# Seven products for a fourth k pair in three FFN down parts, and a tile of sums in the first FFN parts

## The chip, the cores and the metric

The kernel runs on one core of one Trainium2 chip. The metric is the device time of a run in microseconds (us). A core has five engines that run side by side and wait for each other by semaphores: TensorE (PE, matmuls; its weight loads are listed as PEld), VectorE (DVE), ScalarE (ACT), GpSimd (POOL) and SyncE (SP, which here only issues DMAs). VectorE and ScalarE carry out their instructions in the order in which they are written, and so does the DMA queue of SyncE.

## What is computed

A trunk of two layers over 256 positions and 2048 features, in float32. Each layer has a mixer (sliding-window attention and mLSTM in the first, forgetting attention in the second) and a feed-forward net (FFN) of hidden size 5632; the change lies in the FFN alone:

```python
def swiglu(xn, w_gate, w_up, w_down):
    return (jax.nn.silu(xn @ w_gate) * (xn @ w_up)) @ w_down

    for layer in range(DEPTH):
        ...
        h = h + mix.astype(h.dtype)
        h = h + swiglu(rms_norm(h, norm_ffn[layer]), w_gate[layer], w_up[layer], w_down[layer])
    return rms_norm(h, norm_final)
```

## The kernel before

**Products of float32 from two halves.** Every operand is split into a high part and the rest: ScalarE casts (`hi`), VectorE subtracts (`lo`), as in `split_chunk` (L188, L189) and `split_plain` (L357, L358). One product of a 128x128 block of activations (kept in TensorE) with 128x512 weights (streamed) is three matmuls, `three` (L533 to L535): high by high, high by low, low by high.

**Tiles.** Activations are cut into k tiles of 128 features (x in `xh`, `xl`; the FFN's inner values in `mh`, `ml`) and two halves of 128 positions, t0 and t1. Weights are loaded by SyncE in raw tiles of 128 x 2 x 512 float32, 512 KB, which are two neighbouring k tiles (a k pair) of one matrix and 512 of its columns. Split weights go into `hi`/`lo` slots; `slot` hands out eight of them in turn during the FFN.

**A group.** `pair_group` computes two blocks of 512 columns at once: gate and up in a gate/up group, two neighbouring blocks of the output in a down group. It walks over k pairs in a given order, a list of (kind, pair). A pair of kind 0 is plain: two raw tiles, each split whole, and 2 x 2 x 2 = 8 products, 24 matmuls. A pair of kind 1 is mixed: its four blocks of activations and four of weights go through a scheme of the Strassen-Winograd kind, with seven products, 21 matmuls, for which sums of weight blocks and sums of activation blocks are needed. The sums of activations for a pair (`sums_of`) are made once, kept in `sx` or `sd`, and used by every group of the part; both have room for three pairs. A fourth mixed pair exists in four gate/up groups (`HEAVY` for the groups in `DENSE`: 4, 5, 8, 9); its sums lie in `x4` and in the t1 halves of `xh` and `xl` that mixed pairs leave unused, since the scheme reads only t0 of a pair's first k tile. The products that belong to both output blocks gather in four banks of PSUM (`prods`), the others in four more (`plain`); `combine` adds the first up at the end of the last mixed pair, and the two sets of banks change places from group to group.

**Weight sums of a mixed pair**, with raw tiles ra and rb of two k tiles each: ra is split; rb's first half becomes ra's plus rb's first half, by VectorE (L606) in the first part and by an accumulating DMA on POOL's queue (L600) in the others (`adding`); rb is split; L608 and L610 make the other three sums in place in rb and ra; those are split in two steps. Raw tiles of mixed pairs come from a pool with five buffers (`RAWS`), those of plain pairs from one with four (`wr`). `pair_group` has a second form of the sums, with other slots (`halves`), that the mixers use.

**The FFN's stages.** `ffn` runs three parts: gate/up groups 0 to 2, 3 to 6 and 7 to 10, each followed by two down groups (output blocks 0 and 1, then 2 and 3) over the part's 12 or 16 k tiles. The orders are `ORDER` or `HEAVY` for gate/up, `DOWN` for down: two mixed pairs of six in the first part, three of eight in the others (1, 3 and 5). The last part of layer 1 has only its first down group in this form. The output of a gate/up group (SiLU, product) is turned by transposing DMAs on SyncE's queue (L709); `join` then splits it into `mh`, `ml` and makes the sums of its mixed pairs. `join` is due at position 6 of the next gate/up group (`MID`), or at position 5 of the first down group (`MID_DOWN`); so the two last k pairs of a down group come last in its order. The first part's last group is turned on TensorE instead. After a down group its sums are added to h (L768) and then the four plain banks (`close`, L371).

**What sets the order.** The program is written in this order, and a scheduler places each engine's instructions ahead of time by its own estimate of durations, so neighbouring pairs' instructions are interleaved on TensorE, VectorE and ScalarE. On the chip each engine keeps to that order.

Of the kernel before, what the change touches and what calls it, by code (L numbers as in the profile page):

```python
# [24 lines left out]
CK = 2  # L25
# [17 lines left out]
    8: ((0, 0), (1, 1), (0, 2), (1, 3), (0, 4), (1, 5), (0, 6), (0, 7)),  # L43
}
MID = 6
MID_DOWN = 5
# [8 lines left out]
LATER_DOWN = (5, 6)  # L55
RAWS = 5
P_JOIN = 4
# [19 lines left out]
def trunk(  # L77
# [48 lines left out]

    loaded = [None]

    def load_raw(w, k0, c0, n, pool=wr, bufs=4, raws=None):
# [134 lines left out]
    def sums_of(pool, sh, sl, copies, full=None, tags=("tmp", "tmp"), bufs=None, box=None, x4=None):  # L264
        if box is not None:
            full, s = box[:, 0:4, :].rearrange("p (i t) q -> p i t q", i=2), box[:, 4:8, :]
            copies(full.rearrange("p i t q -> p i (t q)"))
        elif full is None:
            full = pool.tile([P, 2, NT, P], F32, tag=tags[0], name="full", bufs=bufs)
            copies(full.rearrange("p i t q -> p i (t q)"))  # L270
        if box is None:
            s = pool.tile([P, 4, P], F32, tag=tags[1], name="s4", bufs=bufs)
        nc.vector.tensor_tensor(out=s[:, 0, :], in0=full[:, 0, 1, :], in1=full[:, 1, 1, :], op=ALU.add)
        nc.vector.tensor_tensor(out=s[:, 1, :], in0=s[:, 0, :], in1=full[:, 0, 0, :], op=ALU.subtract)
        nc.vector.tensor_tensor(out=s[:, 2, :], in0=full[:, 0, 1, :], in1=full[:, 0, 0, :], op=ALU.subtract)
        nc.vector.tensor_tensor(out=s[:, 3, :], in0=full[:, 1, 0, :], in1=s[:, 1, :], op=ALU.subtract)
        if x4 is None:
            split_plain(sh, sl, s)
        else:
            split_plain(sh, sl, s[:, 0:3, :])  # L280
            split_plain(x4[:, 0, :], x4[:, 1, :], s[:, 3, :])
# [63 lines left out]
    def scrap(fp, n):  # L345
# [194 lines left out]
    def pair_group(fp, par, lhs, sums, mats, order, todo=(), halves=None, inner=None, raws=None, adding=False):  # L540
# [32 lines left out]
        for pos, (kind, pair) in enumerate(order):  # L573
# [72 lines left out]
    def ffn(layer, fp, sx, x4, sd, key, todo, idx_next=None, key_next=None, finish=None):  # L646
        r = rstd(key)

        def sums_x(pair):
# [5 lines left out]
        for g0, g1 in zip(PARTS, PARTS[1:]):  # L655
            end = g1 == PARTS[-1]
            nk = 4 * (g1 - g0)
            order = DOWN[nk // 2]
            for g in range(g0, g1):
# [50 lines left out]
                def join(c=c, turned=turned, g=g, g0=g0, order=order):  # L710
                    ct = c[:, 0:2, :].rearrange("p a n -> p (a n)")
# [7 lines left out]
                    for half in range(2):  # L719
                        pair = 2 * (g - g0) + half  # L720
                        if pair in mixed_of(order):
                            j = mixed_of(order).index(pair)
                            sums_of(
                                fp,
                                sd[0][:, j, :, :],
                                sd[1][:, j, :, :],
                                None,
# [24 lines left out]
            for n0 in (0, 2):  # L752
                if end and idx_next is None and n0 == 2:
# [5 lines left out]
                plain, c = pair_group(  # L759
                    fp, 1 - n0 // 2, m_of, sums_d, [(wd, n0 * NB), (wd, (n0 + 1) * NB)], order, todo, adding=g0 >= ADDING  # L760
                )
# [12 lines left out]
    def close_layer(layer, w_out, idx, key, **rest):  # L774
        with tc.tile_pool(name=f"fp{layer}", bufs=2) as fp:
            nx = len(mixed_of(ORDER))
            nd = max(len(mixed_of(o)) for o in DOWN.values())
            sx = [fp.tile([P, nx, 4, P], F32R, name=f"sx{i}", bufs=1) for i in range(2)]
            x4 = fp.tile([P, 2, P], F32R, name="x4", bufs=1)
            todo = out_proj(w_out, idx, key, (*sx, x4, fp))  # L780
            sd = [fp.tile([P, nd, 4, P], F32R, tag=f"sd{i}", name=f"sd{i}", bufs=1) for i in range(2)]
            more = [[fp.tile([P, CK, NB], F32R, name=f"{a}{i}", bufs=1) for a in ("hi", "lo")] for i in range(2)]
            stock.extend(more + [slot() for _ in range(6)])
            ffn(layer, fp, sx, x4, sd, key, todo, **rest)
            stock.clear()


# [599 lines left out]
```

## Time and profile before

| | |
|---|---|
| median of 3 runs | 2088.28 us (2087.98 to 2088.78) |
| the profiled execution's own time | 2086.12 us |
| its span, first to last instruction | 2084.4 us |
| its mean granted TensorE clock | 0.996 |

The profile is of one execution. Its page gives busy times of the engines (the share of the span in which at least one instruction of the engine was under way), the chain of work that ended last, and groups of instructions with their mean duration. A window's row gives, after the length of the stretch, the busy time of TensorE, its weight loads, VectorE, ScalarE and POOL with the number of instructions, then the granted clock, the share of the DMA engines and GB/s. Timeline rows give start, length, engine, line and tiles, and in brackets the idle time before and what ended it. Records of one engine can overlap: an instruction's start, not its end, then tells what it costs.

### The profile page before, as it was taken

The numbers are of one execution on the slowest core, as the hardware profiler recorded it, in microseconds if no ns is written. First come the engines' busy times: TensorE is split into PE (matmuls) and PEld (weight loads), VectorE is DVE, ScalarE is ACT, GpSimd is POOL, SyncE is SP. The second block draws the span as 40 slices with busy tenths as digits, with TensorE's granted clock in tenths as the row PEclk, the third lists the DMA queues.
The fourth block names the chain that finished last, engine by engine and source line by source line (L and its number), as shares of the span: only waits on it lengthen the run. The fifth ranks groups of instructions, "written<-read, shape, count | busy, mean of one in ns | idle before, by whom it ended". The sixth has DMA issues, their size and how long they took to land.

```text
span 2084.4 us, 26995 instructions
## 1 busy us (share of the span) xinstructions
PE 2066.4 (99%) x9449; PEld 1713.1 (82%) x9449; DVE 1804.5 (87%) x2235; ACT 1383.7 (66%) x1760; POOL 113.2 (5%) x143
## 2 busy tenths in 40 slices
PE   9999999999999999999999999999999999999998
PEld 7878887887888888888888888888878888888887
DVE  6788768999899998998899688679998999899994
ACT  6777677765567656767677776687655677557763
POOL 1010000000000000000010000000000000000000
PEclk9999999999999999999999999999999999999999
DMA  8566577666778777778676766587657777867864
GB/s 292 175 208 197 189 252 227 187 204 213 210 225 265 232 233 237 226 240 218 205 211 208 229 198 185 155 265 227 222 174 235 236 220 239 259 205 209 265 206 150
DMA packets 320664, 455.07 MB, mean 218 GB/s; under 512 B 107644, under 2 KB 115856, under 8 KB 320400
## 3 DMA queue, kind: packets, MB, share of 16 engines
q1 hardware_dynamic: 307088, 426.27, 64.9%
q0 software_dynamic: 12720, 25.99, 6.8%
q8 instruction: 74, 1.21, 0.2%
q10 hardware_dynamic: 720, 1.09, 0.2%
q14 instruction: 62, 0.51, 0.1%
HBM read 428.87 MB, written 2.12 MB: 207 GB/s over the span
## 4 chain that ended last, share of the span: by engine, by line
PE 86%; DMA 4%; DVE 4%; ACT 4%; issue 3%; SPq 0%; ACTq 0%; POOLq 0%; POOL 0%; DVEq 0%
PE acc L533 19%; PE acc L534 19%; PE acc L535 19%; PE prod L533 5%; PE prod L534 5%; PE prod L535 5%; PE acc L224 4%; PE acc L223 4%; PE acc L225 4%; DVE lo L189 1%; DMA raw<-in_w_down_dram 1%; ACT hi L188 1%; DMA raw<-in_w_gate_dram 1%; PE p L387 1%; ACT box L323 1%
## 5 line engine op out<-in xcount | busy, mean ns | idle before, releaser
L189 DVE TENSOR_TENSOR lo<-raw,hi 128x1024 fp32r<-128x1024 f32 (+3 forms) x648 | 762.7, 1192 | 148.5 <-ACT hi L188 146.2
L188 ACT CAST hi<-raw 128x1024 fp32r<-128x1024 f32 (+3 forms) x648 | 654.0, 1027 | 352.9 <-PE acc L535 130.1
L534 PE MATMUL acc<-lo,xh 128*128 128x512 f32 x1272 | 495.0, 390 | 0.0
L535 PE MATMUL acc<-hi,xl 128*128 128x512 f32 x1272 | 493.9, 390 | 0.0
L533 PE MATMUL acc<-hi,xh 128*128 128x512 f32 x1272 | 480.5, 391 | 2.4 <-ACT hi L188 2.4
L357 ACT CAST hi<-raw 128x1024 fp32r<-128x1024 f32 (+1 forms) x323 | 286.9, 894 | 193.7 <-DVE raw L608 78.2
L358 DVE TENSOR_TENSOR lo<-raw,hi 128x1024 fp32r<-128x1024 f32 (+1 forms) x323 | 328.3, 1026 | 31.2 <-ACT hi L357 30.4
L533 PEld LDWEIGHTS acc<-hi,xh 128*128 128x128 f32 x1272 | 239.4, 188 | 53.6 <-ACT hi L188 4.0
L534 PEld LDWEIGHTS acc<-lo,xh 128*128 128x128 f32 x1272 | 239.6, 188 | 49.7 <-issue 0.2
L535 PEld LDWEIGHTS acc<-hi,xl 128*128 128x128 f32 x1272 | 239.3, 188 | 49.9
L534 PE MATMUL acc<-lo,mh 128*128 128x512 f32 x466 | 181.4, 390 | 0.0
L535 PE MATMUL acc<-hi,ml 128*128 128x512 f32 x466 | 180.8, 389 | 0.0
L533 PE MATMUL acc<-hi,mh 128*128 128x512 f32 x466 | 176.3, 389 | 4.4 <-ACT hi L357 4.4
L610 DVE TENSOR_TENSOR raw<-raw 128x1024 f32<-128x1024 f32 x103 | 125.6, 1220 | 0.9
L224 PE MATMUL acc<-lo,mh 128*128 128x512 f32 (+1 forms) x322 | 126.3, 392 | 0.0
L223 PE MATMUL acc<-hi,mh 128*128 128x512 f32 (+1 forms) x322 | 125.8, 391 | 0.0
L225 PE MATMUL acc<-hi,ml 128*128 128x512 f32 (+1 forms) x322 | 123.7, 391 | 0.0
L533 PEld LDWEIGHTS acc<-hi,mh 128*128 128x128 f32 x466 | 87.5, 188 | 23.0 <-ACT hi L357 4.9
L534 PEld LDWEIGHTS acc<-lo,mh 128*128 128x128 f32 x466 | 87.6, 188 | 18.2
L535 PEld LDWEIGHTS acc<-hi,ml 128*128 128x128 f32 x466 | 87.6, 188 | 18.2
L224 PE MATMUL acc<-lo,xh 128*128 128x512 f32 (+3 forms) x288 | 99.9, 347 | 0.2 <-DVE lo L189 0.2
L225 PE MATMUL acc<-hi,xl 128*128 128x512 f32 (+3 forms) x288 | 98.8, 344 | 0.0
(362 smaller groups left out, 3033.1 us busy)
## 6 DMA issues: line engine op xcount, KB each, us to landing
raw<-in_w_gate_dram SPq DMA_DIRECT2D x176, 512.0 KB, 5.3
raw<-in_w_up_dram SPq DMA_DIRECT2D x176, 512.0 KB, 5.2
raw<-in_w_down_dram SPq DMA_DIRECT2D x176, 512.0 KB, 5.7
raw<-in_w_in_odd_dram SPq DMA_DIRECT2D x88, 512.0 KB, 5.1
raw<-in_w_in_even_dram SPq DMA_DIRECT2D x51, 512.0 KB, 4.7
raw<-in_w_out_even_dram SPq DMA_DIRECT2D x32, 512.0 KB, 5.1
raw<-in_w_out_odd_dram SPq DMA_DIRECT2D x32, 512.0 KB, 4.7
raw<-in_w_gate_dram POOLq DMA_DIRECT2D x56, 256.0 KB, 5.7
```

Of the source, the lines that this page charges most:

```text
L188: latest[0] = nc.scalar.copy(hi[:, k, 0:n], raw[:, k, 0:n])
L189: nc.vector.tensor_tensor(out=lo[:, k, 0:n], in0=raw[:, k, 0:n], in1=hi[:, k, 0:n].bitcast(F32), op=ALU.subtract)
L223: nc.tensor.matmul(o, ah[:, ts], hi, start=(k == 0), stop=False)
L224: nc.tensor.matmul(o, ah[:, ts], lo, start=False, stop=False)
L225: nc.tensor.matmul(o, al[:, ts], hi, start=False, stop=(k == k_all - 1 and cs.stop == n))
L323: nc.scalar.copy(ju[:, :, b], turned[:, b, :, :, :].rearrange("p k t q -> p (k t q)"))
L357: nc.scalar.copy(dst_h, src)
L358: nc.vector.tensor_tensor(out=dst_l, in0=src, in1=dst_h.bitcast(F32), op=ALU.subtract)
L533: nc.tensor.matmul(o, ah, hi, start=start, stop=False)
L534: nc.tensor.matmul(o, ah, lo, start=False, stop=False)
L535: nc.tensor.matmul(o, al, hi, start=False, stop=stop)
L610: nc.vector.tensor_tensor(out=ra, in0=ra, in1=both, op=ALU.subtract)
```

## The change

Two edits, both in the FFN.

**First parts (groups 0 to 2 and their down groups, both layers).** The five raw tiles are no longer taken in turn from a pool but made once (`ring`). In the first parts four of them take the raw weights, and the fifth is a tile of sums, `t4`. The sums of weights are made in another way: rb's second half is split at once; two sums go to `t4`, two to ra; `t4` and ra are then each split whole. The sums are the same four as before. The later parts go on with `adding` and five raw tiles in turn. The box for turning h in the output projection (`scrap`, n = 1) uses two tiles of the ring.

**Down groups of three later parts** (both in layer 0, the first of the two in layer 1): the order becomes `DOWN_MORE`, with four mixed pairs of eight, 1, 3, 4 and 5. The sums of activations of pair 4 are written to the t1 halves of k tiles 2, 6, 8 and 10 of `mh` and `ml` (`MORE_ROOMS`), which mixed pairs 1, 3, 4 and 5 do not read; they are made in the join of the part's third gate/up group and split in two steps of two sums each.

```diff
+DOWN_MORE = ((0, 0), (1, 1), (1, 3), (0, 2), (1, 4), (1, 5), (0, 6), (0, 7))
+FOURTH_DOWN = 4
+MORE_ROOMS = ((2, 7, 4), (8, 11, 2))
...
-RAWS = 5
...
-        if x4 is None:
+        if isinstance(sh, list):
+            for i, (a, b) in enumerate(zip(sh, sl)):
+                split_plain(a, b, s[:, 2 * i : 2 * i + 2, :])
+        elif x4 is None:
             split_plain(sh, sl, s)
...
-            halves = [fp.tile([P, CK, NB], F32, tag="raw", name="box", bufs=RAWS) for _ in range(2)]
+            halves = ring[2:4]
...
-            ra, rb = (load_raw(w, k0, c0, NB, fp, W_RAWS if halves else RAWS, raws) for w, c0 in mats)
+            ra, rb = (load_raw(w, k0, c0, NB, fp, W_RAWS, raws) for w, c0 in mats)
...
-            if halves is None:
-                if not adding:
-                    nc.vector.tensor_tensor(out=rb[:, 0, :], in0=ra[:, 0, :], in1=rb[:, 0, :], op=ALU.add)
+            if adding:
                 split_plain(hu, lu, rb)
...
+            elif halves is None:
+                t4 = ring[4]
+                split_plain(hu[:, 1, :], lu[:, 1, :], rb[:, 1, :])
+                nc.vector.tensor_tensor(out=t4[:, 0, :], in0=rb[:, 0, :], in1=ra[:, 0, :], op=ALU.add)
+                nc.vector.tensor_tensor(out=t4[:, 1, :], in0=rb[:, 1, :], in1=rb[:, 0, :], op=ALU.subtract)
+                nc.vector.tensor_tensor(out=ra[:, 0, :], in0=t4[:, 0, :], in1=rb[:, 1, :], op=ALU.subtract)
+                nc.vector.tensor_tensor(out=ra[:, 1, :], in0=ra[:, 1, :], in1=ra[:, 0, :], op=ALU.subtract)
+                parts = []
+                for src in (t4, ra):
+                    hs, ls = slot()
+                    split_plain(hs, ls, src)
+                    parts.append((hs, ls))
+                ht = [parts[a][0][:, b, :] for a in range(2) for b in range(2)]
+                lt = [parts[a][1][:, b, :] for a in range(2) for b in range(2)]
...
+        early_ring = ring[0:4]
...
-            order = DOWN[nk // 2]
+            more = nk == 16 and not (end and idx_next is None)
+            order = DOWN_MORE if more else DOWN[nk // 2]
+            kept = [pair for pair in mixed_of(order) if not more or pair != FOURTH_DOWN]
...
+                    raws=ring if g0 >= ADDING else early_ring,
...
-                            j = mixed_of(order).index(pair)
+                            to = [
+                                sd[i][:, kept.index(pair), :, :]
+                                if pair in kept
+                                else [m[:, slice(*at), P:S] for at in MORE_ROOMS]
+                                for i, m in enumerate((mh, ml))
+                            ]
...
-            def sums_d(pair, order=order):
-                j = mixed_of(order).index(pair)
+            def sums_d(pair, kept=kept):
+                if pair not in kept:
+                    return [[m[:, k, P:S] for at in MORE_ROOMS for k in range(*at)] for m in (mh, ml)]
+                j = kept.index(pair)
                 return four(sd[0], j), four(sd[1], j)
...
+            ring.extend(fp.tile([P, CK, NB], F32, name=f"raw{i}", bufs=1) for i in range(5))
             todo = out_proj(w_out, idx, key, (*sx, x4, fp))
```

More of the change, by code (lines that the diff above doesn't have):

```diff
@@ L127, in trunk @@
     loaded = [None]
+    ring = []
     def load_raw(w, k0, c0, n, pool=wr, bufs=4, raws=None):
@@ L709, in ffn, with join @@
                         nc.sync.dma_start_transpose(turned[b][:, :, t, :], flat[:, b, t, :])
-                def join(c=c, turned=turned, g=g, g0=g0, order=order):
+                def join(c=c, turned=turned, g=g, g0=g0, order=order, kept=kept):
                     ct = c[:, 0:2, :].rearrange("p a n -> p (a n)")
@@ L721, in join @@
                         if pair in mixed_of(order):
-                            j = mixed_of(order).index(pair)
+                            to = [
[4 more added lines that the diff above has]
+                            ]
                             sums_of(
                                 fp,
-                                sd[0][:, j, :, :],
-                                sd[1][:, j, :, :],
+                                *to,
                                 None,
@@ L759, in ffn @@
                 plain, c = pair_group(
-                    fp, 1 - n0 // 2, m_of, sums_d, [(wd, n0 * NB), (wd, (n0 + 1) * NB)], order, todo, adding=g0 >= ADDING
+                    fp, 1 - n0 // 2, m_of, sums_d, [(wd, n0 * NB), (wd, (n0 + 1) * NB)], order, todo,
+                    raws=ring if g0 >= ADDING else early_ring, adding=g0 >= ADDING
                 )
@@ L785, in close_layer @@
             stock.clear()
+            ring.clear()
     acc0 = new_acc()
```

## The prediction, made before the result was known

> **What bounds the kernel now.** I read the page's busy times first, then the chain of waits, then windows cut at the FFN's groups, and last the timeline and the wait lists at the few places where TensorE stops.
>
> ```profile
> span 2084.4 us, 26995 instructions
> PE 2066.4 (99%) x9449; PEld 1713.1 (82%) x9449; DVE 1804.5 (87%) x2235; ACT 1383.7 (66%) x1760; POOL 113.2 (5%) x143
> ...
> PE 86%; DMA 4%; DVE 4%; ACT 4%; issue 3%; SPq 0%; ACTq 0%; POOLq 0%; POOL 0%; DVEq 0%
> ```
>
> TensorE is busy 99% of the span and is 86% of the chain, so the number of matmuls sets the time as long as nothing runs short. A matmul's own record is 390 ns, but records overlap, so the price of one is the distance between starts:
>
> ```profile
> 484.10 0.39 PE L533 MATMUL acc<-hi,mh 128*128 128x512 f32 x1
> ...
> 486.14 0.39 PE L533 MATMUL acc<-hi,mh 128*128 128x512 f32 x1
> ```
>
> Nine matmuls lie between these two starts: 2.04 / 9 = 0.227 us each. A plain k pair (24 matmuls) is 5.44 us of TensorE, a mixed one (seven products, 21 matmuls) 4.76.
>
> The engine behind it is VectorE. These windows cover layer 0's second part from its first gate/up group (3) through groups 4, 5, 6 to its two down groups:
>
> ```profile
> 518.00:560.00 42.00, 42.00 (x187) 34.79 (x186) 38.08 (x41) 23.64 (x26) 3.40 (x4) 1.00 0.77 223
> 560.00:606.00 46.00, 46.00 (x204) 38.09 (x203) 41.69 (x48) 30.61 (x34) 3.50 (x5) 1.00 0.77 229
> 606.00:648.00 42.00, 42.00 (x187) 34.75 (x187) 40.60 (x48) 30.72 (x34) 2.59 (x3) 1.00 0.82 238
> 648.00:684.00 36.00, 36.00 (x160) 29.83 (x159) 34.64 (x41) 25.03 (x28) 2.61 (x3) 1.00 0.84 249
> 684.00:725.00 41.00, 41.00 (x182) 33.96 (x181) 36.31 (x39) 27.05 (x30) 2.58 (x3) 1.00 0.79 238
> 725.00:764.00 39.00, 39.00 (x173) 32.29 (x173) 36.60 (x38) 20.77 (x23) 2.59 (x3) 1.00 0.76 236
> ```
>
> After the window's length come TensorE, its weight loads, VectorE, ScalarE. TensorE has no idle time in any of them; VectorE works 227.9 of 246.0 us. The third row matters most: group 5, with four mixed pairs of eight, runs VectorE at 97% and TensorE still never stops.
>
> TensorE does stop in the first parts, which are the ones the diff's other half touches:
>
> ```profile
> 348.00:364.00 16.00, 13.59 (x46) 10.39 (x45) 15.07 (x21) 8.58 (x12) 0.00 (x0) 0.79 0.73 243
> 466.00:480.00 14.00, 11.96 (x56) 9.55 (x55) 12.73 (x15) 9.86 (x12) 0.00 (x0) 1.00 0.68 212
> 1410.00:1420.00 10.00, 9.15 (x39) 6.93 (x39) 10.00 (x15) 7.78 (x11) 0.00 (x0) 1.00 0.60 193
> 1526.00:1540.00 14.00, 11.61 (x47) 9.08 (x46) 12.63 (x14) 9.04 (x11) 0.00 (x0) 0.88 0.78 248
> ```
>
> Length minus matmuls at 0.227 is lost: 5.6, at least 1.3 (2.0 by the wait below), 1.2 and 3.3 us, together about 12. In the first and last row the granted clock fell too (0.79, 0.88), so a stop costs more than itself.
>
> **Down groups: the matmuls removed.** Three parts have two down groups each; every group turns one plain pair into a mixed one, 24 to 21 matmuls. 6 x 3 x 0.227 = **4.1 us less TensorE**. All of it is on the path, since TensorE has no idle time there.
>
> **Down groups: the work added.** VectorE's prices, from the groups by shape (busy, mean ns of one) and from the timeline (start, length):
>
> ```profile
> L189 DVE TENSOR_TENSOR lo<-raw,hi 128x1024 fp32r<-128x1024 f32 x612 | 738.2, 1220 | 138.4 <-ACT hi L188 136.1 <-DMA hv<-room 0.4
> ...
> L610 DVE TENSOR_TENSOR raw<-raw 128x1024 f32<-128x1024 f32 x103 | 125.6, 1220 | 0.9
> ...
> L358 DVE TENSOR_TENSOR lo<-raw,hi 128x512 fp32r<-128x512 f32 x117 | 80.2, 685 | 8.3 <-ACT hi L357 8.3
> ...
> L608 DVE TENSOR_TENSOR raw<-raw 128x512 f32<-128x512 f32 x103 | 70.7, 686 | 0.9
> ```
>
> ```profile
> 714.92 2.35 DVE L189 TENSOR_TENSOR lo<-raw,hi 128x1024 fp32r<-128x1024 f32 x2
> ...
> 729.16 1.88 DVE L371 TENSOR_TENSOR h<-acc,h 128x512 f32<-128x512 f32 x3
> ```
>
> These overlap too: two long ones take 2.35 us (distance 1.13), three short ones 1.88 (distance 0.60). A plain pair is 2 x 1.13 = 2.26 us; a mixed pair with the accumulating DMA (three long splits, L610, one short split, L608) 4 x 1.13 + 2 x 0.60 = 5.72. So +3.46 us a group. ScalarE gains two casts' worth, and it is at 21 to 27 us of about 40. The extra 256 KB accumulating DMA a group goes on POOL, busy 2.6 us of a window:
>
> ```profile
> raw<-in_w_down_dram POOLq DMA_DIRECT2D x21, 256.0 KB, 6.9
> ```
>
> 6.9 us from issue to landing, plus a load of the raw tile, must fit between the split that frees the tile (two mixed pairs earlier) and its use: from the fifth product of pair 3 to the third of pair 5 TensorE takes 2.04 + 5.44 + 4.76 + 1.36 = 13.6 us, so I price it at nothing (without that cover, up to 6.9 us once a group).
>
> The fourth sum is made in the join of the part's third group, which runs in the fourth. Small sums come 0.21 us apart:
>
> ```profile
> 666.02 0.29 DVE L273 TENSOR_TENSOR s<-c 128x128 f32<-128x128 f32 x1 [0.50 <-ACT c L714]
> 666.23 0.28 DVE L275 TENSOR_TENSOR s<-c 128x128 f32<-128x128 f32 x1
> ```
>
> Four of them (0.8) and two splits of 256, which no row shows (between 0.2 and 0.6; I take 0.35, nearer the middle): 1.5 us a part. Per part VectorE gains 2 x 3.46 + 1.5 = 8.4 and goes to 236.3 us, TensorE to 244.6. VectorE still fits with 3.4% over, what group 5 has today.
>
> **Where it does not fit locally.** The new order puts pairs 1 and 3, and 4 and 5, next to each other: 11.4 us of VectorE against 9.5 of TensorE. What carries that is VectorE's lead. Counting splits and matmuls in the program's order, the first split of each down group and the matmul that reads it are:
>
> ```profile
> 674.85 1.22 DVE L189 TENSOR_TENSOR lo<-raw,hi 128x1024 fp32r<-128x1024 f32 x1
> ...
> 683.79 0.39 PE L534 MATMUL acc<-lo,mh 128*128 128x512 f32 x1
> ...
> 725.27 0.39 PE L534 MATMUL acc<-lo,mh 128*128 128x512 f32 x1
> ```
>
> Leads of 7.7 and (714.92 + 1.22 = 716.14) 9.1 us. In the second group VectorE must then do, until the second mixed pair is split: one split 1.13, the rest of combine 0.60 + 1.13, the adds to h 2.26, four closes 2.4, two mixed pairs 11.44, together 18.96. TensorE gets to that pair's fifth product after 5.44 + 4.76 + 2.72 = 12.9. A lead of 6.1 is needed. The new lead is 9.1 - 1.5 - 3.46 - 0.68 = 3.5, plus what VectorE fills of its 4.7 idle us in 684:725: 3.5 to 8.2, so a stop of 0 to 2.6 us. In the first group 18.0 us is due in the same way (1.73 + 1.13, four adds 2.4, two scalings 1.3, 11.44), 5.1 of lead is needed and 7.7 - 1.5 = 6.2 is there, less up to 2 us in which VectorE waits for ScalarE's copies: 0 to 0.9. Per part 0 to 3.5; I take 0.5, near the lower end, because group 5's row shows 97% without a stop. Three parts: **+1.5 us** (0 to +10.5).
>
> **First parts.** 26 mixed pairs (three gate/up groups of three and two down groups of two, in two layers) change form. VectorE: four long and three short before, three long and five short after, 6.32 against 6.39 us, +0.07 each. What shortens is the chain: today L606, cast, split, L608, L610, cast, split follow each other (0.6 + 1.05 + 1.22 + 0.69 + 1.22 + 1.05 + 1.22 = 7.1); afterwards four short sums, cast, split (2.4 + 1.05 + 1.22 = 4.7), and the split of the second tile's upper half waits for nothing but its load. It matters where TensorE waits for the last cast of a mixed pair:
>
> ```profile
> 470.58 1.04 ACT L188 CAST hi<-raw 128x1024 fp32r<-128x1024 f32 x1 [2.02 <-DMA raw<-in_w_down_dram]
> 471.53 0.58 ACT L357 CAST mh<-pf 128x512 fp32r<-128x512 f32 x1
> 472.01 1.05 ACT L357 CAST hi<-raw 128x1024 fp32r<-128x1024 f32 x1
> ...
> 473.11 0.49 PE L533 MATMUL acc<-hi,mh 128*128 128x512 f32 x1 [2.04 <-ACT hi L357]
> ```
>
> That cast is queued behind one that waits for a load; a chain 2 us shorter can slip ahead of it. The same shape stands at 1529. The stop near 354 is a load, which the chain does not cure directly. Of the 12 us lost I take a quarter, **-3 us**; bounds -9.6 (all but the 2.4 idle us in the first row) and +3 (26 x 0.07 = 1.8, and one more stop of 1.2 like the third row's).
>
> The four raw tiles: a pair's first load now waits for the split that its second waited for already, so SyncE's queue stops at the same event one load earlier. What stands behind it is the next plain pair's loads, and behind them ScalarE's casts; cover is the lead above, the price nothing (up to one load a stop, inside the +3).
>
> **The sum.** -4.1 + 1.5 - 3 = -5.6 us. The profiled execution took 2086.12 (1.7 around its span), 2.16 under the runs' median, and would take 2080.5; the median 2088.28 becomes **2082.7 us**.
>
> [...] The distances of 1.13 and 0.60 above disagree with whole durations of 1.22 and 0.69 in a row, and the measurement decides. [...]
>
> **The rivals.**
> *Given back (same).* VectorE loses 2 us a part at the adjacent pairs (6 in all) and the first parts' gain is 0: -4.1 + 6 = +1.9, or with half the gain +0.4; about 2088.7. For it: 3.4% over is an average. Against: group 5's row.
> *First parts unchanged (same).* The stops there are loads; the shorter chain does nothing. -4.1 + 1.5 = 2085.7. For it: the 2.02 us wait for a DMA above; against: TensorE's wait names L357.
> *Slower.* One mechanism: at the second of two adjacent mixed pairs in a down group VectorE's lead is gone, TensorE stops, and its clock falls. Price 3.5 us a part, 10.5, and after each part's stop a slow stretch as after the first row's (5.6 lost, 2.4 of it idle, so 3.2 slow) or none: mean 1.6, 4.8. With half the first parts' gain: -4.1 + 10.5 + 4.8 - 1.5 = +9.7, 2098.0. It decides from 4.1 / 6 = 0.7 us a group on. For it: the lead is down to 7.7 after four gate/up groups; no row shows two mixed pairs in a row. Against: 8.3 us of VectorE left over a part.
> *Whole durations.* If VectorE's instructions did not overlap, a down group would be 4 x 2.44 + 4 x 6.25 + combine, adds and closes 7.8 = 42.6 us against TensorE's 40.8, +1.8 x 6 - 4.1 = +6.7, 2095. The same sum forbids today's group 5. [...]
>
> **How the numbers follow.** Forecast 0.42 (own range 2077 to 2084), given back 0.16, first parts unchanged 0.10, slower 0.29, whole durations 0.03. Faster by over 0.2% (4.2 us, about what a measurement of this kernel can tell from no change) 0.42, same 0.26, slower 0.32. The low end is -4.1 with the first parts near -7, 2077; the high end, 2097, stops just short of the slower case's full price.
>
> **What would show it.** In the down groups: 18 fewer matmuls, TensorE busy the whole window and VectorE at 96 to 99%. A stop of over 0.7 us before a matmul on a lo or hi of the second adjacent pair speaks for the slower case. In the first parts: the four windows lose less than 12 us; if the wait before the down group's matmul still names L357 with a load ahead, that step is wrong. A gap on a load in groups that have none now would make the tile count, which I priced at nothing, the error.

## The result and the profile after

| | before | after |
|---|---|---|
| median | 2088.31 us (2087.98 to 2088.78, 4 runs) | 2197.77 us (2194.39 to 2199.49, 4 runs) |
| ratio, 95% interval | | 1.0522 (1.0504 to 1.0540) |
| span of the profiled execution | 2084.4 us | 2192.7 us |
| mean granted clock | 0.996 | 0.985 |

The changed kernel is 5.2% slower, 109.5 us by the medians. The forecast was 2082.7 us in a range of 2077 to 2097, so even the range missed it. From the page of the changed kernel, its busy times, the chain of waits and ScalarE's casts of raw tiles outside the plain pairs:

```profile
span 2192.7 us, 26987 instructions
...
PE 2108.7 (96%) x9431; PEld 1715.9 (78%) x9431; DVE 1831.0 (84%) x2303; ACT 1393.4 (64%) x1778; POOL 113.2 (5%) x149
...
PE 54%; DMA 18%; DVE 16%; issue 7%; ACT 6%; SPq 0%; POOL 0%; POOLq 0%; ACTq 0%; DVEq 0%
...
L363 ACT CAST hi<-raw 128x512 fp32r<-128x512 f32 (+1 forms) x341 | 301.2, 893 | 312.8 <-DMA raw<-in_w_gate_dram 65.8
```

The 18 matmuls are gone (9431 against 9449) and VectorE has 26.5 us more to do, close to the 27 priced (three parts of 8.4 and 1.8 in the first parts). But TensorE's idle time, span less busy, went from 18.0 to 84.0 us, and its busy time rose by 42.3 us although it has less to do. Those are the 108.3 us by which the span grew: 66.0 of plain standing still, and 42.3 in which the matmuls' records still cover the time: matmuls at half the clock (115 pairs of starts are 0.40 to 0.46 us apart in this trace, 37 in that of before, 78 x 0.2 = 16 us) and waits, or the first part of longer ones, that lie under a record of 0.39 us. The chain of waits is no longer TensorE's (86% before, 54% now); transfers and VectorE have 34% of it.

The first parts are not where it happened. Windows of the changed kernel there (length, then busy time of TensorE, its weight loads, VectorE, ScalarE, POOL, then clock, DMA share, GB/s):

```profile
340.00:360.00 20.00, 19.23 (x85) 15.59 (x85) 19.20 (x27) 16.43 (x23) 0.00 (x0) 1.00 0.70 234
460.00:480.00 20.00, 20.00 (x91) 15.83 (x90) 19.17 (x23) 12.33 (x15) 0.00 (x0) 1.00 0.77 233
1460.00:1480.00 20.00, 18.92 (x84) 15.36 (x83) 19.47 (x31) 19.80 (x30) 0.00 (x0) 1.00 0.71 210
1580.00:1600.00 20.00, 19.57 (x89) 15.37 (x88) 18.84 (x24) 12.48 (x15) 0.00 (x0) 1.00 0.62 202
```

TensorE idles 2.3 us in the four together, and the clock stays at 1.00; the prediction counted some 12 us lost at these places before. The later parts have it, for example in the first two down groups of four mixed pairs (about 683 to 786 us by the count of matmuls; the first two rows lie in them) and in the gate/up groups behind them (third row):

```profile
680.00:721.00 41.00, 34.94 (x140) 27.42 (x139) 32.94 (x37) 24.87 (x29) 1.72 (x2) 0.92 0.68 177
721.00:765.00 44.00, 39.62 (x157) 31.01 (x155) 30.87 (x33) 16.68 (x20) 3.25 (x4) 0.88 0.56 171
...
822.00:871.00 49.00, 47.40 (x200) 38.08 (x200) 41.88 (x49) 30.93 (x35) 3.47 (x4) 0.97 0.75 224
```

In the first two rows VectorE is busy 80% and 70% of the window, where 96 to 99% was forecast, and the transfers have thinned out as well. No engine is at its limit here; they wait for each other. The wait lists (total us, times, longest) say for what, before and after:

```profile
ACT hi L357 <- DMA raw<-in_w_gate_dram: 6.4, 4, 1.9
ACT hi L357 <- DMA raw<-in_w_down_dram: 5.3, 4, 1.7
```

```profile
ACT hi L363 <- DMA raw<-in_w_gate_dram: 65.8, 24, 7.2
...
ACT hi L363 <- DMA raw<-in_w_down_dram: 65.2, 19, 10.7
```

Casts of mixed pairs' raw tiles wait 131 us for transfers, 11.7 before. One such wait, from the timeline of the changed kernel:

```profile
688.40 2.95 DVE L364 TENSOR_TENSOR lo<-raw,hi 128x512 fp32r<-128x512 f32 x3
...
691.38 0.37 SPq L138 DMA_DIRECT2D raw<-in_w_down_dram  x1
...
696.29 0.86 POOL L606 DMA_DIRECT2D raw<-in_w_down_dram  x1 [16.50 <-DMA raw<-in_w_down_dram]
...
702.53 1.99 ACT L363 CAST hi<-raw 128x1024 fp32r<-128x1024 f32 x2 [5.30 <-DMA raw<-in_w_down_dram]
...
703.62 0.80 PE L539 MATMUL prod<-hi,mh 128*128 128x512 f32 x1 [4.81 <-ACT hi L363]
704.22 0.63 PE L540 MATMUL acc<-lo,mh 128*128 128x512 f32 x1
```

Three splits of an earlier mixed pair end at 691.35. Only then can the next raw tile be loaded (691.38). When it has landed, POOL issues the accumulating transfer (696.29); when that has landed, ScalarE casts (702.53), and TensorE goes on after 4.81 idle us (703.62). From that split to the cast lie 11.2 us that the tile spends in two transfers one after the other, and TensorE had run out of work 7.5 us after the split (703.62 - 4.81 - 691.35). From the second one (704.22) on, the matmuls after the stop are some 0.43 us apart instead of 0.227:

```profile
703.60:708.90 5.30, 5.28 (x12) 4.15 (x13) 4.47 (x5) 3.76 (x4) 0.00 (x0) 0.50 0.26 56
```

Twelve matmuls in 5.30 us at a granted clock of 0.50 cost 2.6 us on top of the stop. The Trainium skill ("TensorE: Matmul & The Clock Gate", Part 1: The HAM clock gate) has the clock halved after an idle window of about 3.4 us and back after a busy one of the same length. The stop of 4.81 us agrees with the first half; the slow stretch is longer than one such window. And shorter stops do it too: two of 1.82 and 1.98 us, with 1.75 us of matmuls between them, stand ahead of this row of the same kernel:

```profile
745.30:751.00 5.70, 5.10 (x11) 3.61 (x12) 5.70 (x8) 2.29 (x3) 0.00 (x0) 0.50 0.00 0
```

### The profile page after: what moved, and what is told of

Same layout as the page of the kernel before. It is cut to its first block, busy times and chain, and to the rows that moved or that the text cites. A ratio compares the mean times of both kernels' runs of the same rounds, so it can differ in the third digit from the quotient of the medians.

```text
span 2192.7 us, 26987 instructions
## 1 busy us (share of the span) xinstructions
PE 2108.7 (96%) x9431; PEld 1715.9 (78%) x9431; DVE 1831.0 (84%) x2303; ACT 1393.4 (64%) x1778; POOL 113.2 (5%) x149
## 4 chain that ended last, share of the span: by engine, by line
PE 54%; DMA 18%; DVE 16%; issue 7%; ACT 6%; SPq 0%; POOL 0%; POOLq 0%; ACTq 0%; DVEq 0%
PE acc L541 11%; PE acc L540 11%; PE acc L539 11%; DMA raw<-in_w_gate_dram 7%; DMA raw<-in_w_down_dram 6%; DVE lo L364 5%; DVE lo L192 4%; PE acc L227 4%; PE acc L226 4%; PE acc L228 4%; DMA raw<-in_w_up_dram 3%; PE prod L540 3%; PE prod L541 3%; PE prod L539 3%; ACT hi L363 2%
## 5 line engine op out<-in xcount | busy, mean ns | idle before, releaser
L192 DVE TENSOR_TENSOR lo<-raw,hi 128x1024 fp32r<-128x1024 f32 (+3 forms) x642 | 755.1, 1192 | 148.5 <-ACT hi L191 146.1
L191 ACT CAST hi<-raw 128x1024 fp32r<-128x1024 f32 (+3 forms) x642 | 645.8, 1025 | 321.9 <-PE acc L541 113.6
L363 ACT CAST hi<-raw 128x512 fp32r<-128x512 f32 (+1 forms) x341 | 301.2, 893 | 312.8 <-DMA raw<-in_w_gate_dram 65.8
L539 PE MATMUL acc<-hi,xh 128*128 128x512 f32 x1272 | 486.6, 394 | 1.3 <-ACT hi L191 1.2
L364 DVE TENSOR_TENSOR lo<-raw,hi 128x512 fp32r<-128x512 f32 (+1 forms) x341 | 346.4, 1027 | 117.5 <-ACT hi L363 117.1
L540 PE MATMUL acc<-lo,mh 128*128 128x512 f32 x436 | 174.1, 400 | 10.0 <-DVE lo L192 8.3
L539 PE MATMUL acc<-hi,mh 128*128 128x512 f32 x436 | 166.4, 400 | 15.3 <-ACT hi L363 9.2
L541 PE MATMUL acc<-hi,ml 128*128 128x512 f32 x436 | 171.8, 396 | 0.5 <-DVE ml L364 0.5
L540 PEld LDWEIGHTS acc<-lo,mh 128*128 128x128 f32 x436 | 83.2, 191 | 32.2 <-DVE lo L192 12.7
L614 DVE TENSOR_TENSOR raw<-raw,raw 128x1024 f32<-128x1024 f32 x83 | 101.0, 1220 | 0.5
```

The costliest lines, as they stand in the source:

```text
L191: latest[0] = nc.scalar.copy(hi[:, k, 0:n], raw[:, k, 0:n])
L192: nc.vector.tensor_tensor(out=lo[:, k, 0:n], in0=raw[:, k, 0:n], in1=hi[:, k, 0:n].bitcast(F32), op=ALU.subtract)
L363: nc.scalar.copy(dst_h, src)
L364: nc.vector.tensor_tensor(out=dst_l, in0=src, in1=dst_h.bitcast(F32), op=ALU.subtract)
L539: nc.tensor.matmul(o, ah, hi, start=start, stop=False)
L540: nc.tensor.matmul(o, ah, lo, start=False, stop=False)
```

## The experiments

Three theories stood at first. **A:** raw tiles handed out in a fixed turn (`ring`) make a mixed pair's second raw tile wait for a later split than the pool of before did, and the way of that tile (load, accumulating transfer, cast, splits) is then too long. **B:** the new order of the down groups, two mixed pairs next to each other, outruns VectorE (the prediction's slower rival). **C:** the scheduler places the instructions in another order.

**1. Three mixed pairs again, tiles in turn.** The changed kernel without the fourth mixed pair.

```diff
-            more = nk == 16 and not (end and idx_next is None)
+            more = False
```

> The changed kernel with DOWN's three mixed pairs of eight in every later part; the ring of five tiles in turn stays. Theory A (tiles in turn: a mixed pair's second raw tile is the one that the first raw tile of two pairs earlier leaves, so its load waits for that pair's last split instead of the short split before it, and a load, an accumulating DMA, and the splits behind them make a loop of about 18 us over two mixed pairs): gate/up groups 4, 5, 8, 9 with four mixed pairs still stop, about half of the 109 us stays, 2120 to 2170. Theory B (down order: VectorE has no lead at two adjacent mixed pairs): all of it goes, 2083 to 2090.

Measured 2112.80 us (2110.68 to 2119.46), ratio 1.0128 (1.0108 to 1.0149). That is outside the ranges of both theories: most of the loss goes, and some stays.

**2. Own tiles, four mixed pairs.** In the later parts first raw tiles go round three tiles, second ones round two.

```diff
+        own = (ring[0::2], ring[1::2])
-                    raws=ring if g0 >= ADDING else early_ring,
+                    raws=own if g0 >= ADDING else early_ring,
```

> The changed kernel with its four mixed pairs in down, but in the later parts first raw tiles take three of the five ring tiles in turn and second raw tiles the other two, so that a second tile waits for the short split of the second tile two pairs earlier. Theory A: nearly all of the 109 us goes, 2080 to 2100; what stays over 2085 is the down order's own. Theory B: no change, 2190 to 2200. Theory C (another placing of instructions because tiles are no longer from a pool): no change either.

Measured 2145.34 us (2140.22 to 2146.11), ratio 1.0274 (1.0258 to 1.0289). No theory's range has that either: A alone does not explain the loss, and neither does B.

**3. Both.** What remains of the change is the first parts' form and the own tiles.

> Both: own tiles for first and second raw tiles, and three mixed pairs in down; against before only the first parts' form differs. Theory A and B: 2080 to 2088, the first parts' own gain (their stops were 12 us before and look like 3 in the changed kernel's trace, so about 2079). Theory C: well above 2090.

Measured 2076.17 us (2074.82 to 2077.68), ratio 0.9948 (0.9932 to 0.9965): faster than both kernels. With the change itself these make a table of two by two:

| | three mixed pairs in down | four |
|---|---|---|
| own tiles | 2076.17 | 2145.34 |
| tiles in turn | 2112.80 | 2197.77 |

The turn costs 36.6 us with three mixed pairs and 52.4 with four; the fourth pair costs 69.2 us with own tiles and 85.0 in turn. Each is a loss by itself. Theory C alone is out, since it had run 3 well above 2090. The turn can be seen at work in the timelines of the two kernels with three pairs, at the same mixed pair. First in turn (SPq are SyncE's load issues):

```profile
570.95 0.69 DVE L364 TENSOR_TENSOR lo<-raw,hi 128x512 fp32r<-128x512 f32 x1
571.67 0.37 SPq L138 DMA_DIRECT2D raw<-in_w_gate_dram  x1
...
572.69 1.22 DVE L364 TENSOR_TENSOR lo<-raw,hi 128x1024 fp32r<-128x1024 f32 x1
...
572.80 1.51 SPq L138 DMA_DIRECT2D raw<-in_w_up_dram  x2
```

then with own tiles:

```profile
569.63 0.69 DVE L364 TENSOR_TENSOR lo<-raw,hi 128x512 fp32r<-128x512 f32 x1
...
570.35 1.50 SPq L138 DMA_DIRECT2D raw<-in_w_up_dram  x2
```

The short split frees the second raw tile, the long one the first. So it was with the pool of before:

```profile
518.17 0.69 DVE L358 TENSOR_TENSOR lo<-raw,hi 128x512 fp32r<-128x512 f32 x1
...
518.89 0.37 SPq L135 DMA_DIRECT2D raw<-in_w_up_dram  x1
```

There and with own tiles the short split lets the next pair's *second* tile be loaded, the `up` block, the one that the accumulating transfer must still follow. In turn it lets the first be loaded, and `up` comes 2 us later, after the long split (the second of the two loads in the last row of run 1, which starts at 573.94). It is not these three rows alone. From 500 to 1000 us and from 1560 to 1960 us, which hold nearly all of the later parts, the gate and up loads that start within 0.12 us of the end of a short split are `up` blocks 44 times and `gate` blocks never in the kernel before and with own tiles (run 3); in turn (run 1) they are `gate` blocks 41 times and an `up` block once. So the pool of before did not hand its tiles out in a fixed turn, as the section on the change has it, and the turn takes the early load of `up` away.

The first parts gained. The same places in the kernel with own tiles and three pairs (all of layer 1 comes earlier there):

```profile
340.00:360.00 20.00, 20.00 (x89) 16.54 (x89) 19.33 (x27) 16.21 (x23) 0.00 (x0) 1.00 0.74 242
460.00:480.00 20.00, 20.00 (x91) 15.78 (x90) 19.12 (x24) 12.29 (x14) 0.00 (x0) 1.00 0.74 235
1400.00:1420.00 20.00, 18.85 (x83) 15.28 (x82) 19.57 (x29) 16.05 (x24) 0.00 (x0) 1.00 0.76 265
1500.00:1540.00 40.00, 39.88 (x179) 32.13 (x178) 38.34 (x46) 21.70 (x25) 0.91 (x1) 1.00 0.61 194
```

1.3 us are idle there at a clock of 1.00, where about 12 were lost before, which is the 11.0 us (from 2087.14, the kernel before measured beside it, to 2076.17) within a microsecond. Three of the four stops are gone; the third place still loses 1.15 us, as much as before (1.2). The rest of the study is the fourth pair's 69 us. In the kernel with own tiles and four pairs, one of the first stops looks like this:

```profile
692.68 0.86 POOL L609 DMA_DIRECT2D raw<-in_w_down_dram  x1 [23.44 <-DVE lo L192]
...
699.65 1.05 ACT L363 CAST hi<-raw 128x1024 fp32r<-128x1024 f32 x1 [2.72 <-DMA raw<-in_w_down_dram]
...
700.73 1.23 DVE L364 TENSOR_TENSOR lo<-raw,hi 128x1024 fp32r<-128x1024 f32 x1 [2.54 <-ACT hi L363]
```

From the issue of the accumulating transfer to the cast 7.0 us pass, and VectorE stands idle for 2.54 of them. That suggested latency (L) against work (V) as the next question.

**4. Alternating order in the second down groups.**

```diff
+DOWN_APART = ((1, 1), (0, 0), (1, 3), (0, 2), (1, 4), (0, 6), (1, 5), (0, 7))
-..., order, todo,
+..., DOWN_APART if more and n0 else order, todo,
```

> Own tiles and four mixed pairs in down, as in e2_own_tiles, but in the second down group of each of the three parts mixed and plain pairs alternate. Two neighbouring pairs then give TensorE 5.44 + 4.76 = 10.2 us for one mixed pair everywhere in that group, where the changed order has 14.96 us for two of them; the work of every engine is the same. Theory L (latency: a mixed pair's second raw tile must be loaded, added to by the second transfer, cast and split before the next load can start, and that takes longer than TensorE's time for the pairs between): the second groups' stops go, about half of the 69 us that four mixed pairs cost with own tiles, 2105 to 2120. Theory V (VectorE or ScalarE has too much work in a down group, in whatever order): no more than 10 us of it goes, 2135 to 2145.

Measured 2144.57 us (2139.42 to 2145.92), ratio 1.0264 (1.0244 to 1.0283): 0.8 us from run 2, and in theory V's range. The time is the same, but it is not lost at the same places. The second down group of layer 0's second part and the two gate/up groups behind it, in run 2:

```profile
725.00:770.00 45.00, 40.95 (x174) 33.20 (x173) 37.04 (x39) 20.20 (x23) 2.59 (x3) 0.96 0.69 207
770.00:867.00 97.00, 91.46 (x393) 74.10 (x392) 86.60 (x95) 56.57 (x63) 6.92 (x8) 0.98 0.73 211
```

and here:

```profile
724.00:764.00 40.00, 39.72 (x173) 31.71 (x172) 34.61 (x37) 20.59 (x23) 3.46 (x4) 1.00 0.73 217
764.00:867.00 103.00, 93.27 (x390) 72.46 (x389) 85.37 (x94) 54.14 (x61) 6.94 (x8) 0.97 0.71 210
```

Pulled apart, the pairs no longer stop TensorE in their own group (0.3 idle us against 4.1), but the groups behind lose what was saved (9.7 against 5.5): 10.0 us in all against 9.6. By the starts of matmuls, layer 1's part does the same; in layer 0's last part the rearranged group itself loses more. So here the order decides where TensorE stops and not how much it loses. Neither theory B, which put the loss down to the adjacent pairs, nor L in this form expects that.

**5. The first parts' form in the down groups.**

```diff
-                    raws=own if g0 >= ADDING else early_ring, adding=g0 >= ADDING
+                    raws=early_ring if more or g0 < ADDING else own, adding=g0 >= ADDING and not more
```

> As e2_own_tiles, but the four mixed pairs of the later parts' down groups take the first parts' new form: four short sums on VectorE in place of the accumulating transfer and of two of the differences, four raw tiles in turn and the tile of sums. VectorE's work in a down group grows by about 4 x 0.6 = 2.4 us and one transfer of about 7 us leaves each mixed pair's way. Theory L: most of the 69 us goes, 2072 to 2090. Theory V: VectorE gets more to do, slower than e2_own_tiles by 6 x 2.4 = 14 us, about 2160.

Measured 2138.62 us (2137.69 to 2140.95), ratio 1.0241 (1.0225 to 1.0257). 6.7 us better than run 2, far from either theory's number. It also brings the fixed turn back, on four tiles, so it does not say what the transfer alone costs.

**6. VectorE makes the first sum; tiles and order of pairs as in run 2.**

```diff
+                if adding == 2:
+                    nc.vector.tensor_tensor(out=rb[:, 0, :], in0=ra[:, 0, :], in1=rb[:, 0, :], op=ALU.add)
-                    ..., adding=g0 >= ADDING
+                    ..., adding=2 if more else g0 >= ADDING
```

> As e2_own_tiles, with one thing undone alone: in the down groups of four mixed pairs VectorE forms the first sum with one short instruction (0.69 us, 0.60 in a row) instead of the accumulating transfer; tiles, order, casts and splits stay. VectorE's work grows by 4 x 0.60 = 2.4 us a group. Theory L: 6.8 to 7.9 us leave each mixed pair's way, and with them most of the 69 us: 2076 to 2095. Theory V: slower than e2_own_tiles, about 2160. A third theory, S (the loads themselves are late, because SyncE's queue holds four transposing transfers of 1.2 to 2 us each at the start of the down groups, and everything queued behind them lands in a bunch): the stops stay on loads that are not followed by an accumulating transfer, 2110 to 2145.

Measured 2111.46 us (2109.84 to 2114.53), ratio 1.0115 (1.0095 to 1.0134). Without the accumulating transfers, all four of each of these groups and not the fourth pair's alone, 33.9 of the 69.2 us go, although VectorE has more to do; 35 stay. Neither L nor V has that: the transfers' time counts, and it is not all. The number lies at the low end of theory S's range; its sign, stops on plain loads, is not there in the first two of these groups, where ScalarE's casts wait 2.8 us in all for loads (677 to 760 us). S was not followed further.

**7. Four pairs, VectorE relieved.**

```diff
+            if light:
+                return c
-                for t in range(NT):
+                for t in range(0 if more else NT):
-                    add_out(acc, n)
+                    if not more:
+                        add_out(acc, n)
```

> As e2_own_tiles (own tiles, four mixed pairs in down, accumulating transfers), but VectorE is relieved in the down groups of the three later parts: the combining of the four products (0.69 + 1.22 us), the two adds to h (2 x 1.22) and, in the two parts that don't end a layer, the four adds of the plain sums (4 x 0.69 a part) are left out, 4.3 to 5.7 us a group. TensorE's, ScalarE's and the transfers' work is as before; VectorE has less to do in such a part than in e3_own_three. Theory L (latency of a mixed pair's tiles, the accumulating transfer of 6.8 to 7.9 us above all, with VectorE idle while it waits): the work was not the limit, 2125 to 2145. Theory V (VectorE's work is so near to TensorE's time that any wait of its own, for a cast or a transfer, comes out as a stop): with 10% of slack the stops go, 2070 to 2090.

This kernel leaves out the combining and the adds to h in these groups, so it does not compute the trunk; it only shows what their time is worth. Measured 2096.82 us (2095.17 to 2097.16), ratio 1.0046 (1.0029 to 1.0063), between the two theories and nearer to V. 48.5 us go with transfers and tiles as they were, for 34.0 us less of busy VectorE by the pages; 21 stay.

**8. Three pairs, VectorE loaded with idle work.**

```diff
+            if pos == 4:
+                for _ in range(pad):
+                    o = h[:, 0, 0 : 2 * NB]
+                    nc.vector.tensor_tensor(out=o, in0=o, in1=o, op=ALU.max)
```

> As e3_own_three (own tiles, three mixed pairs in down), with VectorE's part of a fourth mixed pair put in as work that does nothing: ahead of the fifth pair of each later down group four (first group) or three (second) long instructions that take the maximum of a part of h with itself, 7 x 1.13 = 7.9 us a part against the 8.4 us of the fourth pair and its sums. No load, cast, split or transfer is added or moved. Theory V: about the loss of e2_own_tiles, 2125 to 2150. Theory L: little or nothing, 2074 to 2090. Where both count, the two runs of this call land between.

Measured 2112.95 us (2106.62 to 2118.04), ratio 1.0121 (1.0094 to 1.0148). But the scheduler had moved the idle work. The row of that line (shortest, median and longest ns, first and last start):

```profile
L584 DVE TENSOR_TENSOR h<-h x21: 1215/1222/1226, 489.9 to 1822.8; 128x1024 f32<-128x1024 f32 x21
```

It begins at 490 us, ahead of the part it was meant for, so this run says only that 21 long instructions of VectorE cost 37 us somewhere.

**9. The same work, held in place.**

```diff
-                    nc.vector.tensor_tensor(out=o, in0=o, in1=o, op=ALU.max)
+                    with tc.issue_after(low[0].ins):
+                        nc.vector.tensor_tensor(out=o, in0=o, in1=o, op=ALU.max)
```

> As e9_three_padded, whose idle long instructions the scheduler had placed as early as 490 us, ahead of the part they were meant for: here each is queued behind VectorE's latest split of a mixed pair, so that the 7 x 1.13 = 7.9 us a part lie inside the down groups. Theory V (VectorE's work next to its limit there): 2100 to 2150. Theory L (the way of the mixed pair's tiles, not the work): 2074 to 2090. Theory C (it is neither, but another order of instructions by the scheduler): any value, and then the two nudged kernels of this call move as well.

Measured 2123.96 us (2123.39 to 2127.11), ratio 1.0176 (1.0161 to 1.0191): 47.8 us for 21 x 1.13 = 23.7 us of work, in theory V's range. No load, cast or transfer was added. Where it comes out is the surprise; windows of this kernel:

```profile
680.00:720.00 40.00, 39.91 (x177) 32.73 (x176) 36.17 (x36) 24.48 (x27) 2.59 (x3) 1.00 0.80 238
720.00:760.00 40.00, 40.00 (x178) 33.14 (x177) 36.61 (x38) 20.72 (x23) 2.60 (x3) 1.00 0.70 214
...
800.00:840.00 40.00, 35.93 (x153) 29.11 (x152) 29.54 (x32) 20.37 (x23) 2.59 (x3) 0.97 0.78 220
...
1000.00:1040.00 40.00, 33.33 (x132) 24.80 (x131) 33.68 (x42) 22.23 (x35) 0.87 (x1) 0.91 0.46 125
```

The padded down groups of layer 0's second part (first two rows) lose 0.1 us. The gate/up groups behind them, which hold no padding, lose about 4 us in a window, with VectorE busy for 29.54 of 40. The last row shows that this is not so everywhere: in the second padded group of layer 0's last part TensorE stops at once. Counted by the starts of matmuls against run 3, some 35 of the 48 us lie behind the padded groups and some 13 in them. The timeline of the third row:

```profile
815.72 6.51 SPq L741 DMA_TRANSPOSE turned<-c  x4
822.33 0.53 SPq L138 DMA_DIRECT2D raw<-in_w_gate_dram  x1
...
829.69 0.86 POOL L615 DMA_DIRECT2D raw<-in_w_gate_dram  x1 [21.12 <-DMA raw<-in_w_up_dram]
...
836.67 1.04 ACT L364 CAST hi<-raw 128x1024 fp32r<-128x1024 f32 x1 [7.46 <-DMA raw<-in_w_gate_dram]
...
837.77 0.79 PE L540 MATMUL prod<-hi,xh 128*128 128x512 f32 x1 [4.07 <-ACT hi L364]
```

The four turning transfers hold SyncE's queue until 822.23, the loads behind them start at 822.33, the accumulating transfer is issued at 829.69, the cast follows at 836.67. TensorE gets there 4.07 us early. The added work had used up the lead in the down groups. That can be counted, run 3 first, then this one, each from group 3 to the same matmul at the end of the two down groups:

```profile
510.10:756.00 245.90, 245.90 (x1086) 203.63 (x1085) 227.56 (x248) 158.16 (x173) 17.27 (x20) 1.00 0.80 237
```

```profile
510.60:756.90 246.30, 246.21 (x1087) 203.61 (x1086) 229.47 (x248) 155.69 (x171) 16.43 (x19) 1.00 0.78 231
```

VectorE has been busy 1.9 us longer, 7.9 us of it with idle work, so it is some 6 us further behind with its own. In the third row the stop came at the next place where loads, an accumulating transfer and casts stand behind one another.

**10 and 11. Nudges.** Against theory C: one short idle instruction in each later down group, on run 3 and on run 2 (`pad=1`, 128 elements).

> As e3_own_three with one short instruction of some 0.3 us (a maximum of 128x128 of h with itself) in each of the six down groups of the later parts, 2 us of VectorE in all, only so that the scheduler places anew: of VectorE's 2263 instructions 2245 keep a common order. Theories V and L: 2074 to 2080, as e3_own_three. Theory C: 2085 or more.

Measured 2076.50 us (2075.82 to 2078.43), 0.3 from run 3.

> The same nudge on e2_own_tiles (four mixed pairs in down): of VectorE's 2305 instructions 2287 keep a common order. Theories V and L: 2138 to 2152, as e2_own_tiles. Theory C: under 2130 or over 2160.

Measured 2145.07 us (2142.93 to 2147.36), 0.3 from run 2. A slightly different placing moves nothing; a larger one was not tried by itself.

**Taken together.** VectorE's share of a later part can be estimated from the prediction's own windows (227.9 of 246.0 us, 244.6 with four pairs) and a third of the difference of the pages' busy times. Those lines, run 3 first, then 2, 6, 7 and 9, each from its own page:

```profile
PE 2062.2 (99%) x9449; PEld 1710.5 (82%) x9449; DVE 1805.2 (87%) x2261; ACT 1385.3 (67%) x1760; POOL 115.3 (6%) x143
```

```profile
PE 2087.5 (97%) x9431; PEld 1712.1 (80%) x9431; DVE 1829.0 (85%) x2303; ACT 1391.9 (65%) x1778; POOL 116.5 (5%) x149
```

```profile
PE 2076.6 (99%) x9431; PEld 1708.8 (81%) x9431; DVE 1840.7 (87%) x2327; ACT 1395.6 (66%) x1778; POOL 94.7 (4%) x125
```

```profile
PE 2069.2 (99%) x9431; PEld 1709.0 (82%) x9431; DVE 1795.0 (86%) x2257; ACT 1394.2 (67%) x1778; POOL 114.5 (5%) x149
```

```profile
PE 2077.0 (98%) x9449; PEld 1711.6 (81%) x9449; DVE 1827.0 (86%) x2282; ACT 1382.7 (65%) x1760; POOL 109.9 (5%) x143
```

| run | mixed pairs, transfers in down | VectorE's share of a later part | median |
|---|---|---|---|
| 3 | three, accumulating | 228.1 / 246.0 = 92.7% | 2076.17 |
| 7 | four, accumulating | 224.7 / 244.6 = 91.9% | 2096.82 |
| 6 | four, none | 240.0 / 244.6 = 98.1% | 2111.46 |
| 9 | three, accumulating | 235.4 / 246.0 = 95.7% | 2123.96 |
| 2 | four, accumulating | 236.1 / 244.6 = 96.5% | 2145.34 |

From run 3 to run 9 only VectorE's work was added (21.8 us by the pages), from 7 to 2 too (34.0 us): 48 us each. At nearly the same share, from 3 to 7 and from 9 to 2, the fourth pair's tiles and transfers cost 21 us each, net of the 4 us of matmuls that they save. So both count. They do not simply add, though: run 6, with the highest share of all but without the transfers, is 34 us faster than run 2.

Two things stay open. Runs 6, 7 and 9 are placed anew by the scheduler to a larger extent than the nudges (by the names of their tiles, 8899 of the 9449 matmuls of run 9 keep a common order with run 3, and 9409 of the nudged run 10), so some of their differences may be placing; the kernels with and without the turn also differ in it. And that the turning transfers on SyncE's queue are what makes the late stops late is read from the trace and was not tried; the kernel before has them too, 5.11 to 6.28 us at a time in the later parts of layer 0, and does not stop there.

## Why the prediction was wrong

- **Matmuls removed, -4.1 us.** Right in count; it could not come out, because TensorE's matmuls alone no longer set the end.
- **VectorE's added work, 8.4 us a part.** Right in size: the page has 26.5 us more in all, of which 1.8 were forecast for the first parts, 8.2 a part. The step that failed is the sentence after it, "VectorE still fits with 3.4% over, what group 5 has today". Group 5 has 97% for 42 us, and the two gate/up groups ahead of it have 91%, so it can live on a lead that they leave. In a whole part at 96% the lead is used up and not rebuilt in time (runs 4 and 9 show the loss moving on to the groups behind): work alone cost 48 us, for 21.8 us of it in run 9 and 34.0 in run 7.
- **The extra accumulating transfer, priced at nothing.** Failed. The step compared one transfer of 6.9 us and a load with 13.6 us of TensorE between the split that frees the tile and its use. The size of the transfers was right: the load, the accumulating transfer and the cast's wait took 11.2 us at the first long stop. The cover was not: it was worked out for engines that run on time, and TensorE ran out of work 7.5 us after that split. Without the transfers of all four pairs 33.9 of 69.2 us went (run 6); no run leaves out the extra one alone.
- **The stop at adjacent mixed pairs, +1.5 us (0 to +10.5).** Far too small, and only part of the place. By the starts of matmuls, run 2 loses some 39 us against run 3 in its six down groups and 29 more in the groups behind them. Pulling the pairs apart in half the groups moved stops and saved nothing beyond noise (0.8 us, run 4). The step counted what each group lacks and left out that the lead is still missing in the next one.
- **The raw tiles.** "The four raw tiles", priced at nothing, held in the first parts. What the prediction did not price at all is that the later parts' five tiles change from a pool, in which the short split frees the tile for the next `up` block, to a fixed turn, in which the long split does. That was 36.6 to 52.4 us. The last part of the prediction did name the sign of it: a gap on a load in groups that had none.
- **First parts, -3 us (-9.6 to +3).** The mechanism was right and its size was off: with the rest undone the kernel gains 11.0 us, more than the bound of 9.6. Three of the four stops vanish, also the one near 354 that was put down to a load: in run 3 the mixed pair's last long cast starts at 349.74, ahead of the cast that waits for a load, where before it starts at 356.35 behind it. The third stop stays.
- **The slower rival (0.29)** had its mechanism half right, VectorE's lead and the falling clock, but not only at the adjacent pairs, and its price of 10.5 + 4.8 us was far too low: it let each stop stand by itself.

So the prediction failed by taking each edit's cover as still there once the others were in, and by not seeing the turn at all. The better kernel is the change without its down half: the first parts' tile of sums, own tiles in the later parts and three mixed pairs, 0.9948 (0.9932 to 0.9965) of the time before.

## What to carry to other kernels

When a buffer pool becomes a fixed turn, write down for each tile which instruction frees its predecessor: the number of tiles can stay the same while the one with the longest way behind it is freed last. An engine that is second in line with 7% over is not idle in any useful sense; that slack is what absorbs transfers, and taking half of it can cost more than the work put in (here 48 us for 24). When a stop goes away and the time stays, look for it in the groups behind. Price a transfer at nothing only if its cover still stands when the engine that frees its buffer runs late.

## What the hardware showed

The accumulating transfers of 256 KB have a median of 6.0 us (gate/up 5.0) from issue to landing in the changed kernel, but in a stop ScalarE, and behind it VectorE and TensorE, wait for them: 7.0 us from issue to cast at 692.68 in run 2 and 836.67 - 829.69 = 7.0 in run 9. A stop of 4.81 us brought twelve matmuls at half the clock, and 78 more matmuls than before ran so, 16 us of the loss beside the idle time. One such long stop is not needed: stops of 1.82 and 1.98 us close together were followed by the same clock of 0.50.
